# Gate steps of a PEER layer: both one-hots in one tile, a ring of three blocks, one of them taken from the weights' low parts

## The chip, the core and the metric

The kernel runs on one core of a Trainium2 chip. The metric is device time in microseconds for one execution. The profile names the engines PE (matrix products), PEld (its weight loads), DVE (vector), ACT (scalar), POOL (GpSimd) and SP (whose queue issues most loads).

## The reference

One decoder layer for 1024 prompt tokens and 64 sample tokens: RMSNorm, one input projection that feeds a retention group and an RWKV-7 group, an output projection, then a PEER mixer and a gated per-layer embedding (PLE). The part that the change touches is the PEER mixer:

```python
q = (xb @ wq).reshape(PEER_BLOCK, PEER_HEADS, 2, PEER_DKEY // 2)
s = jnp.einsum('phcd,hcnd->phcn', q, keys).astype(jnp.float32)
sv, si = lax.top_k(s, PEER_TOPK)
cand = sv[:, :, 0, :, None] + sv[:, :, 1, None, :]
cv, ci = lax.top_k(cand.reshape(PEER_BLOCK, PEER_HEADS, PEER_TOPK * PEER_TOPK), PEER_TOPK)
e = (jnp.take_along_axis(si[:, :, 0], ci // PEER_TOPK, axis=-1) * PEER_NKEYS
     + jnp.take_along_axis(si[:, :, 1], ci % PEER_TOPK, axis=-1))
gsm = jax.nn.softmax(cv, axis=-1)
hval = jnp.einsum('pd,phkd->phk', xb, u_tab[e])
act = (jax.nn.gelu(hval.astype(jnp.float32), approximate=False) * gsm).astype(xb.dtype)
return jnp.einsum('phk,phkd->pd', act, v_tab[e])
```

Every token picks 8 x 16 = 128 of 16384 experts. An expert's number is a pair (i, j) of two numbers below 128.

## The kernel before

The tokens are nine tiles of up to 128. Five of them (`E0` = 0, 1, 8 and `G1` = 2, 3) go the sparse way: `gather` (L1131) fetches 128 rows of `pu` and then 128 rows of `pv` for each token by indirect DMAs that POOL issues (L1141), and DVE multiplies and adds them (L1155, L1169). The other four (`G2` = 4, 5, 6, 7, together 512 tokens) go the dense way: all 16384 experts are computed for all of them, and a gate, zero for most pairs, picks.

The dense way has these parts.

- `hidden` (L1270) is one of 128 units, one for each number i. SP loads a block `uraw` of 128 x 1024 (L1274, ring `UB` = 2). `split` (L296) makes a high part `uh` on ACT (L298) and a low part `ul` on POOL (L302), each from a ring of `DW` = 4 blocks of 4 KB a partition. `mm3` (L324) makes the product in three passes of eight: high by high (L327), high by low of the tokens (L328), and last low by high (L330), which is the one reader of `ul`. A gelu goes on to `gd` in DRAM for the first `NPRE` = 96 units, or stays in PSUM for the others.
- `gates` (L1241) makes the gate matrix of a tile, 32 steps for each of four tiles, so 128 steps. A step (L1253 to L1262) takes four tokens. DVE builds two one-hots of 128 x 512, `oh[0]` for the first number of the pair and `oh[1]` for the second (L1256), ACT scales the four parts of `oh[0]` by the softmax (L1258), PE multiplies the two for each token into a PSUM tile `pwt` (L1261, ring of 2, each product two records), and ACT evacuates it into `wst` (L1262). After 16 steps `wst` goes to `wd` in DRAM (L1268); the last half stays on chip. The one-hots come from two tags, `oh0` and `oh1`, with two blocks of 2 KB each, in the pool `gw`.
- `dense_fused` (L1322) runs the last 32 units and multiplies each by its gate (`act`, L1284: L1292 and L1293 on DVE, which need all gate steps done) and by `pv` (`dense`, L1299: products `py`, L1312 to L1315, whose `vh` and `vl` come from ACT and POOL). `dense_stored` (L1341) does the same for the 96 stored units. Beside it `ple_weights` (L1361) loads the weights of the last stage, PLE, into the blocks that the units' rings leave.

The pool `da` (L1485, L1486) holds the rings `uh`, `ul` and `uraw`: 4 + 4 + 2 = 10 blocks of 4 KB. The same rings serve `c_query` (L1009), which runs before the gates, and the last `c_rows` (L574), which puts eight blocks of `w_out` into them.

The loop at L1525 sets the program order: for each dense tile its `topk` (L1044) side by side with the gate steps of the tile before, then a share of the 96 units, then the next tile's gates are set up. `topk` and `gather` of tile 2 are written in its second turn, those of tile 3 in its fifth. The order on each engine is then made by the framework's scheduler, which takes the operations in this order as a priority, runs them against a simulated timeline and lets an engine take what is ready there (L1566). On the chip each engine and each DMA queue works through its list in that fixed order, and a block is handed on when its last reader is done (`reuse_waits="tile"`).

Of the kernel before, what the change touches and what calls it, by code (L numbers as in the profile page):

```python
# [17 lines left out]
D = 1024  # L18
# [159 lines left out]
E0 = [0, 1, 8]  # L178
G1 = [2, 3]
DW = 4  # L180
CN = 2
BORDER = [1, 8, 2, 3, 4, 5, 6, 7]
A0 = [0, 1]
# [29 lines left out]
class K:  # L213
# [360 lines left out]
    def c_rows(self, wp, t, ring=4, da=None, x=None):  # L574

        nc, I = self.nc, self.I
        n = SIZE[t]
        half = lambda name: wp.tile([128, 512], F32, name=name, tag="x2k", bufs=ring)
        cs = [slice(0, 512), slice(512, 1024)]
        if da is not None:  # L580
            ws = []
            for k in range(8):
                ws.append(da.tile([128, D], F32, name="cw", tag=("uh", "ul")[k % 2], bufs=DW))
                nc.sync.dma_start(ws[k], I['w_out'][k])
        if da is not None:
            h = da.tile([128, D], F32, name="ch", tag="uraw", bufs=UB)
        else:
            h = wp.tile([128, D], F32, name="ch", tag="sr", bufs=1)
        nc.sync.dma_start(h[:n], I['x'][t * 128:t * 128 + n])
        yield  # L590
        ot = [half("cot"), self.tail if t == 7 else half("cot")]
        oT = [wp.tile([128, 4, 128], F32, name="coT", tag="qm", bufs=2) for _ in range(2)]
        for k in range(1 if t == 7 else 2):
            nc.sync.dma_start(ot[k][:n], self.od[t][:n, cs[k]])
        yield
        for k in range(2):
            p = self.ps("etr", "a").rearrange("p (a b) -> p a b", a=4)
            for j in range(4):
                nc.tensor.transpose(p[:, j, :n], ot[k][:n, j * 128:j * 128 + 128], self.c("ident")[:n, :n])
            nc.scalar.activation(oT[k][:, :, :n], p[:, :, :n], AF.Copy)  # L600
            yield
        if da is not None:
            p = [self.ps("ewo", "b") for _ in range(2)]
            for k in range(8):
                for c in range(2):
                    nc.tensor.matmul(p[c][:n], oT[k // 4][:, k % 4, :n], ws[k][:, cs[c]], start=k == 0, stop=k == 7)
            for c in range(2):
                nc.vector.tensor_tensor(h[:n, cs[c]], p[c][:n], h[:n, cs[c]], op=OP.add)
        else:
            for c in range(2):  # L610
                p = self.ps("ewo", "a")
                for k in range(8):
                    w = half("cw")
                    nc.sync.dma_start(w, I['w_out'][k, :, cs[c]])
                    nc.tensor.matmul(p[:n], oT[k // 4][:, k % 4, :n], w, start=k == 0, stop=k == 7)
                    if k % 4 == 3:
                        yield
                nc.vector.tensor_tensor(h[:n, cs[c]], p[:n], h[:n, cs[c]], op=OP.add)
        nc.scalar.dma_start(self.hd[t][:n], h[:n])
        junk = wp.tile([128, D], BF, name="csq", tag="x2k", bufs=ring)  # L620
        ssq = wp.tile([128, 1], F32, name="cssq")
        nc.scalar.activation(junk[:n], h[:n], AF.Square, accum_out=ssq[:n])
        r = self.rsq(wp, ssq, n, 1.0 / D, 1e-6, 1, "crs")
        gr = [half("cgr") for _ in range(2)]
        o = ROWS['norm_ffn'][0]
        for c in range(2):
            nc.sync.dma_start(gr[c], I['rows'][o + 512 * c:o + 512 * c + 512].partition_broadcast(128))
            nc.vector.scalar_tensor_tensor(h[:n, cs[c]], h[:n, cs[c]], r[:n], gr[c][:n], op0=OP.mult, op1=OP.mult)
        if x is not None:
            self.split_T(h, n, x[0], x[1], 0)  # L630
        else:
            nc.scalar.dma_start(self.xd[t][:n], h[:n])
        self.rowed.add(t)
        yield
# [374 lines left out]
    def c_query(self, wp, da, parts):  # L1009

        nc, I = self.nc, self.I
        for hc in range(16):
            kT = wp.tile([128, 128], F32, name="keysT")
            nc.sync.dma_start(kT, I['keysT'][:, hc])
            raw = da.tile([128, 8, 128], F32, name="wqr", tag="uraw", bufs=UB)
            nc.sync.dma_start(raw, I['wq'][hc])
            wh = da.tile([128, 8, 128], F32R, name="wqh", tag="uh", bufs=DW)
            wl = da.tile([128, 8, 128], F32R, name="wql", tag="ul", bufs=DW)
            self.split(wh, wl, raw, "g")
            for tiles, x in parts:  # L1020
                off, n = spans(tiles)
                s = wp.tile([128, len(tiles), 128], F32, name=f"ss{tiles[0]}", bufs=SB)
                p = self.ps("pq", "b")
                self.mm3(p[:, :n], lambda k: wh[:, k, :], lambda k: wl[:, k, :], lambda k: x[0][:, k], lambda k: x[1][:, k], 8)
                qT = wp.tile([128, n], F32, name=f"qT{tiles[0]}", bufs=1)
                nc.scalar.activation(qT, p[:, :n], AF.Copy)
                p = self.ps("psc", "a")
                for i, t in enumerate(tiles):
                    nc.tensor.matmul(p[:SIZE[t], i * 128:i * 128 + 128], qT[:, off[t]:off[t] + SIZE[t]], kT, start=True, stop=True)
                nc.scalar.activation(s, p[:, :len(tiles) * 128].rearrange("p (t k) -> p t k", k=128), AF.Copy)  # L1030
                for i, t in enumerate(tiles):
                    self.pick(self.found[t], hc, s[:, i], 128)
            yield
# [204 lines left out]
        for t in E0[1:]:  # L1238
            yield from self.gather(wp, t, rows + ("xT",) * (t == E0[-1]), acc=self.acc)

    def gates(self, wp, t):  # L1241
        nc = self.nc
        n, o = SIZE[t], self.off[t]
        p = self.ps("pit", "i").rearrange("p (a b) -> p a b", a=4)
# [5 lines left out]
        for s in range(0, n, 64):  # L1250
            last = (o + s) // 64 == self.ntok // 64 - 1
            st = self.stage[(o + s) // 64 % 2].tile([128, 128, 64], F32, name="wst", bufs=1)
            for b in range(0, 64, 4):  # L1253
                oh = [wp.tile([128, 4, 128], F32, name=f"oh{j}", bufs=2) for j in range(2)]
                for j in range(2):
                    nc.vector.tensor_tensor(oh[j], io, p[:, j, s + b:s + b + 4, None].to_broadcast([128, 4, 128]), op=OP.is_equal)  # L1256
                for j in range(4):
                    nc.scalar.activation(oh[0][:, j], oh[0][:, j], AF.Copy, scale=it[:, s + b + j:s + b + j + 1])  # L1258
                pw = self.ps("pwt", "w").rearrange("p (a b) -> p a b", a=4)
                for j in range(4):  # L1260
                    nc.tensor.matmul(pw[:, j, :], oh[1][:, j, :], oh[0][:, j, :], start=True, stop=True)  # L1261
                nc.scalar.activation(st[:, :, b:b + 4].rearrange("p i t -> p t i"), pw, AF.Copy)  # L1262
                yield
            if last:
                self.wl = st
                return
            for q in range(0, 128, WQ):
                nc.scalar.dma_start(self.wd[(o + s) // 64, :, q:q + WQ], st[:, q:q + WQ])  # L1268

    def hidden(self, dp, ep, x, i1):  # L1270
# [2 lines left out]
        raw = dp.tile([128, 8, 128], F32, name="uraw", bufs=UB)  # L1273
        nc.sync.dma_start(raw, I['puT'][i1])  # L1274
        uh = dp.tile([128, 8, 128], F32R, name="uh", bufs=DW)
        ul = dp.tile([128, 8, 128], F32R, name="ul", bufs=DW)
        self.split(uh, ul, raw, "g")
        p = self.psh.tile([128, self.ntok], F32, name="ph")
        self.mm3(p, lambda k: uh[:, k, :], lambda k: ul[:, k, :], lambda k: x[0][:, k], lambda k: x[1][:, k], 8)
# [81 lines left out]
    def ple_weights(self, cx, da, dl):  # L1361
        nc, I = self.nc, self.I
        kc = self.ntok // 128
        names = [n for n, b in (("uraw", UB), ("uh", DW), ("ul", DW)) for _ in range(b)]
        self.pg, self.pp = [], []
        for j in range(2):
            a = cx.tile([128, kc, 1024], F32R, name="pga", tag=f"cx{j}")
# [2 lines left out]
        for r, n in ((self.pp, 2), (self.pg, 8)):  # L1370
            for k in range(n):
                for j in range(2):
                    if len(r[j]) <= k:
                        if names:
                            tag = names.pop()
                            r[j].append(da.tile([128, 1024], F32R, name="pgb", tag=tag, bufs=UB if tag == "uraw" else DW))
                        else:
                            r[j].append(dl.tile([128, 1024], F32R, name="pgx", bufs=2))
        for w, src, n in ((self.pp, 'pproj', 2), (self.pg, 'pgate', 8)):
# [57 lines left out]
    def build(self):  # L1437
# [3 lines left out]
        with self.es:  # L1441
# [41 lines left out]
            cx = sb("cx2", ex)  # L1483
            x = self.rows_of(cx, G2)
            da = sb("dna", eg, bufs=2)  # L1485
            self.layout(da, [("uh", [128, 8, 128], F32R, DW), ("ul", [128, 8, 128], F32R, DW), ("uraw", [128, 8, 128], F32, UB)])  # L1486
            tp = sb("tk", et)
            self.found = {t: (tp.tile([128, 16, 16], F32, name=f"sv{t}"), tp.tile([128, 16, 16], U32, name=f"si{t}")) for t in G1 + G2}
            self.e12 = {}
# [26 lines left out]
            with ExitStack() as e:  # L1516
# [1 line left out]
                self.psh = self.pool("psumh", bufs=3, space=PS, es=e, reuse_waits="tile")  # L1518
                gw = sb("gw", e, side="right")
                self.stage = (gw, kp)  # L1520
                self.layout(gw, [("oh0", [128, 4, 128], F32, 2), ("oh1", [128, 4, 128], F32, 2), ("it", [128, 128], F32, 2)])
                gh = sb("gh", e, bufs=2, side="right")
                gate = iter(())
                nh = 0
                for i, t in enumerate(G2 + [None]):  # L1525
# [5 lines left out]
                    while nh < NPRE * (i + 1) // (len(G2) + 1):  # L1531
                        self.nc.scalar.dma_start(self.gd[nh], self.hidden(da, gh, x, nh))
                        nh += 1
                    gate = self.gates(gw, t) if t is not None else gate
                    for t in G1:
                        if i == TK1[t]:
                            run(self.topk(tp, t))
# [32 lines left out]
```

## Time and profile before

| | us |
|---|---|
| median of three runs | 3825.01 |
| lowest and highest of them | 3814.94, 3841.18 |
| the profiled execution's own time | 3810.91 |
| its span, first to last instruction | 3809.0 |

| engine | busy us | share of the span |
|---|---|---|
| PE | 3309.1 | 87% |
| PEld | 2745.7 | 72% |
| DVE | 2966.1 | 78% |
| ACT | 1228.1 | 32% |
| POOL | 2368.8 | 62% |

The shares are means over stages with different limits, so the profile is read by stage. Times inside the execution count from the first instruction. A row of a stage gives the busy time of each engine in it. A row of a group gives its busy time and the mean of one instruction in ns, then the idle time of the engine just before such instructions and what ended it. A row of the timeline gives start, length, engine, line and operation, and in brackets the idle time before it and its end. Matmuls overlap, so one takes longer than the distance to the next. The gate steps lie between 2084 and 2700 us, with a pause from 2165 to 2290. The first 96 units lie between 1940 and 2610 us, the others end at 3019 us.

### The profile page before, as it was taken

What the parts mean: (1) busy time and instruction counts of PE and PEld (TensorE: products, weight loads), DVE (VectorE), ACT (ScalarE), POOL (GpSimd) and SP (SyncE); (2) the same over time, 40 slices, a digit from 0 to 9 for tenths busy, and PEclk for the clock granted to TensorE, in tenths of its full rate; (3) what the DMA queues carried; (4) which work ended last, traced back from release to release, by engine and by line L of the source; (5) the groups of instructions that cost most, each with busy time, mean ns of one, the idle gap of its engine ahead of it and who ended that gap; (6) DMA issues with size and microseconds to landing.
All of it is one profiled execution on the core that took longest, in us unless ns stands there. A gap on an engine that the chain in (4) does not pass through costs nothing. (4 is left out here: it accounts for less than half of the span.)

```text
span 3809.0 us, 52675 instructions
## 1 busy us (share of the span) xinstructions
PE 3309.1 (87%) x17749; PEld 2745.7 (72%) x17749; DVE 2966.1 (78%) x5858; ACT 1228.1 (32%) x2273; POOL 2368.8 (62%) x2059
## 2 busy tenths in 40 slices
PE   7799995868769978875998999998799989899979
PEld 7698994645747757664887778887688877677857
DVE  5454488878897798876998978977877877788885
ACT  4232221111112111211333626778433333333322
POOL 5363176445465375545469898875688788877740
PEclk9799995668878567877999999998899999999989
DMA  7266568889878878888678889898999999999972
GB/s 253 77 221 213 175 197 293 272 296 325 262 245 312 309 265 289 281 305 311 199 271 310 299 296 321 302 361 320 328 346 334 345 371 362 365 366 351 339 247 74
DMA packets 429896, 1086.23 MB, mean 285 GB/s; under 512 B 46971, under 2 KB 146041, under 8 KB 424954
## 3 DMA queue, kind: packets, MB, share of 16 engines
q0 software_dynamic: 165888, 604.05, 44.9%
q1 hardware_dynamic: 205406, 382.77, 30.7%
q10 hardware_dynamic: 58332, 96.03, 6.9%
q8 instruction: 141, 2.31, 0.2%
q14 instruction: 129, 1.06, 0.1%
HBM read 986.68 MB, written 95.94 MB: 284 GB/s over the span
## 5 line engine op out<-in xcount | busy, mean ns | idle before, releaser
L1141 POOL DMA_INDIRECT grow<-in_pv,eid x576 | 572.8, 994 | 465.3 <-DVE gacc L1169 258.9
L1141 POOL DMA_INDIRECT grow<-in_pu,eid x576 | 571.9, 993 | 413.4 <-DVE grow L1155 228.0
L1169 DVE SCALAR_TENSOR_TENSOR gacc<-grow,ac,gacc 128x1024 f32<-128x1024 f32 x571 | 731.6, 1281 | 61.9 <-DMA grow<-in_pv,eid 55.9
L1155 DVE SCALAR_TENSOR_TENSOR grow<-grow,gacc 128x1024 f32<-128x1024 f32 x576 | 690.0, 1211 | 91.5 <-DMA grow<-in_pu,eid 87.9
L1312 PE MATMUL py<-ah,vh 128*128 128x512 f32 x1024 | 405.9, 397 | 31.5 <-ACT vh L298 21.9
L327 PE MATMUL ph<-cx,uh 128*128 128x512 f32 x1024 | 410.9, 401 | 12.6 <-ACT geh L1281 6.9
L328 PE MATMUL ph<-cx,uh 128*128 128x512 f32 x1024 | 407.2, 398 | 0.0
L1313 PE MATMUL py<-al,vh 128*128 128x512 f32 x1024 | 402.9, 394 | 2.9 <-DVE al L300 2.7
L302 POOL TENSOR_TENSOR vl<-vraw,vh 128x640 fp32r<-128x640 f32 (+2 forms) x224 | 326.2, 1461 | 39.9 <-ACT vh L298 21.9
L302 POOL TENSOR_TENSOR ul<-uraw,uh 128x1024 fp32r<-128x1024 f32 x128 | 307.7, 2404 | 60.3 <-ACT uh L298 50.8
L1315 PE MATMUL py<-ah,vl 128*128 128x512 f32 x1024 | 275.5, 400 | 16.7 <-POOL vl L302 15.6
L330 PE MATMUL ph<-cx,ul 128*128 128x512 f32 x1024 | 260.3, 393 | 6.0 <-POOL ul L302 6.0
L1312 PEld LDWEIGHTS py<-ah,vh 128*128 128x128 f32 x1024 | 194.6, 190 | 82.9 <-ACT vh L298 28.8
L298 ACT ACTIVATE vh<-vraw 128x640 fp32r<-128x640 f32 (+2 forms) x224 | 154.6, 693 | 306.9 <-PE py L1313 94.4
L1315 PEld LDWEIGHTS py<-ah,vl 128*128 128x128 f32 x1024 | 193.2, 190 | 66.8 <-POOL vl L302 24.7
L327 PEld LDWEIGHTS ph<-cx,uh 128*128 128x128 f32 x1024 | 196.5, 192 | 58.3 <-ACT uh L298 8.8
L1319 DVE TENSOR_TENSOR yT<-yT,py 128x512 f32<-128x512 f32 x216 | 147.4, 683 | 105.8 <-PE py L1315 80.4
L1313 PEld LDWEIGHTS py<-al,vh 128*128 128x128 f32 x1024 | 194.3, 190 | 47.2 <-DVE al L300 5.5
L328 PEld LDWEIGHTS ph<-cx,uh 128*128 128x128 f32 x1024 | 196.3, 192 | 40.0
L330 PEld LDWEIGHTS ph<-cx,ul 128*128 128x128 f32 x1024 | 190.7, 189 | 46.5 <-POOL ul L302 7.9
L298 ACT ACTIVATE uh<-uraw 128x1024 fp32r<-128x1024 f32 x128 | 135.6, 1059 | 253.2 <-DMA uraw<-in_puT 134.1
L1256 DVE TENSOR_TENSOR oh<-csta,pit 128x512 f32<-128x512 f32 x256 | 161.3, 679 | 49.3 <-PE pwt L1261 42.6
(402 smaller groups left out, 7422.9 us busy)
## 6 DMA issues: line engine op xcount, KB each, us to landing
uraw<-in_puT SPq DMA_DIRECT2D x128, 512.0 KB
vraw<-in_pvd SPq DMA_DIRECT2D x152, 320.0 KB
cw<-in_w_out SPq DMA_DIRECT2D x128, 256.0 KB
wd<-wst ACTq DMA_DIRECT2D x28, 1024.0 KB
wt<-wd SPq DMA_DIRECT2D x64, 448.0 KB
wraw<-in_w_ret SPq DMA_DIRECT2D x48, 512.0 KB
ewq<-in_wq SPq DMA_DIRECT2D x48, 512.0 KB
gd<-geh ACTq DMA_DIRECT2D x96, 256.0 KB
```

The costliest lines, as they stand in the source:

```text
L298: nc.scalar.activation(hi, src, AF.Copy)
L302: nc.gpsimd.tensor_tensor(lo, src, hi.bitcast(F32), op=OP.subtract)
L327: mm(out, lh(k), rh(k), start=first and k == 0, stop=False)
L328: mm(out, *((ll(k), rh(k)) if right else (lh(k), rl(k))), start=False, stop=False)
L330: mm(out, *((lh(k), rl(k)) if right else (ll(k), rh(k))), start=False, stop=last and k == nk - 1)
L1141: nc.gpsimd.indirect_dma_start(out=g, out_offset=None, in_=src, in_offset=bass.IndirectOffsetOnAxis(ap=self.eid[t][:, j:j + 1], axis=0))
L1155: nc.vector.scalar_tensor_tensor(g[:, c], g[:, c], 1.0, x[:, c], op0=OP.mult, op1=OP.mult, accum_out=hv[:, i, j:j + 1])
L1169: nc.vector.scalar_tensor_tensor(y[:, c], g[:, c], ac[:, j:j + 1], y[:, c], op0=OP.mult, op1=OP.add)
L1256: nc.vector.tensor_tensor(oh[j], io, p[:, j, s + b:s + b + 4, None].to_broadcast([128, 4, 128]), op=OP.is_equal)
L1312: nc.tensor.matmul(p, vh[:, b, :], ah, start=b == 0, stop=False)
L1313: nc.tensor.matmul(p, vh[:, b, :], al, start=False, stop=False)
L1315: nc.tensor.matmul(p, vl[:, b, :], ah, start=False, stop=b == nb - 1)
```

## The change

Both one-hots of a step become one tile of 4 KB, `oh`, of shape 128 x 2 x 4 x 128. Two such blocks lie in `gw`, in the room of the four smaller ones. Every third step takes a third block, tag `spare`, from `da`. `da` gives up one block of `ul` for it: `LW` = 3 in place of `DW` = 4. So `ul` is a ring of three everywhere that it is used: in `hidden`, in `c_query`, and in the last `c_rows`, whose eighth `w_out` block goes to `spare`. `ple_weights` takes `spare` as the first of its ten blocks.

```diff
+LW = 3
...
-                ws.append(da.tile([128, D], F32, name="cw", tag=("uh", "ul")[k % 2], bufs=DW))
+                ws.append(da.tile([128, D], F32, name="cw", **(dict(tag="spare", bufs=1) if k == 7 else dict(tag=("uh", "ul")[k % 2], bufs=(DW, LW)[k % 2]))))
...
-            wl = da.tile([128, 8, 128], F32R, name="wql", tag="ul", bufs=DW)
+            wl = da.tile([128, 8, 128], F32R, name="wql", tag="ul", bufs=LW)
...
-    def gates(self, wp, t):
+    def gates(self, wp, t, extra):
...
-                oh = [wp.tile([128, 4, 128], F32, name=f"oh{j}", bufs=2) for j in range(2)]
+                if self.turn % 3 == 2:
+                    oh = extra.tile([128, 2, 4, 128], F32, name="oh", tag="spare", bufs=1)
+                else:
+                    oh = wp.tile([128, 2, 4, 128], F32, name="oh", bufs=2)
+                self.turn += 1
                 for j in range(2):
-                    nc.vector.tensor_tensor(oh[j], io, p[:, j, s + b:s + b + 4, None].to_broadcast([128, 4, 128]), op=OP.is_equal)
+                    nc.vector.tensor_tensor(oh[:, j], io, p[:, j, s + b:s + b + 4, None].to_broadcast([128, 4, 128]), op=OP.is_equal)
                 for j in range(4):
-                    nc.scalar.activation(oh[0][:, j], oh[0][:, j], AF.Copy, scale=it[:, s + b + j:s + b + j + 1])
+                    nc.scalar.activation(oh[:, 0, j], oh[:, 0, j], AF.Copy, scale=it[:, s + b + j:s + b + j + 1])
                 pw = self.ps("pwt", "w").rearrange("p (a b) -> p a b", a=4)
                 for j in range(4):
-                    nc.tensor.matmul(pw[:, j, :], oh[1][:, j, :], oh[0][:, j, :], start=True, stop=True)
+                    nc.tensor.matmul(pw[:, j, :], oh[:, 1, j, :], oh[:, 0, j, :], start=True, stop=True)
...
-        ul = dp.tile([128, 8, 128], F32R, name="ul", bufs=DW)
+        ul = dp.tile([128, 8, 128], F32R, name="ul", bufs=LW)
...
-        names = [n for n, b in (("uraw", UB), ("uh", DW), ("ul", DW)) for _ in range(b)]
+        bufs = dict(uraw=UB, uh=DW, ul=LW, spare=1)
+        names = [n for n in bufs for _ in range(bufs[n])]
...
-            self.layout(da, [("uh", [128, 8, 128], F32R, DW), ("ul", [128, 8, 128], F32R, DW), ("uraw", [128, 8, 128], F32, UB)])
+            self.layout(da, [("uh", [128, 8, 128], F32R, DW), ("ul", [128, 8, 128], F32R, LW), ("uraw", [128, 8, 128], F32, UB), ("spare", [128, 8, 128], F32, 1)])
...
-                self.layout(gw, [("oh0", [128, 4, 128], F32, 2), ("oh1", [128, 4, 128], F32, 2), ("it", [128, 128], F32, 2)])
+                self.turn = 0
+                self.layout(gw, [("oh", [128, 2, 4, 128], F32, 2), ("it", [128, 128], F32, 2)])
```

More of the change, by code (lines that the diff above doesn't have):

```diff
@@ L1375, in ple_weights @@
                             tag = names.pop()
-                            r[j].append(da.tile([128, 1024], F32R, name="pgb", tag=tag, bufs=UB if tag == "uraw" else DW))
+                            r[j].append(da.tile([128, 1024], F32R, name="pgb", tag=tag, bufs=bufs[tag]))
                         else:
@@ L1533, in build @@
                         nh += 1
-                    gate = self.gates(gw, t) if t is not None else gate
+                    gate = self.gates(gw, t, da) if t is not None else gate
                     for t in G1:
```

## The prediction

> **What bounds the kernel now.** I read the page first, then busy time by stage, then the gate steps (L1253 to L1262) in those stages, then who waits for whom, and last the timeline around one hidden unit (`hidden`, L1270).
>
> ```profile
> span 3809.0 us, 52675 instructions
> 2080.00:2170.00 90.00, 85.84 (x441) 71.29 (x440) 88.95 (x163) 60.64 (x126) 80.39 (x59) 1.00 0.90 308
> 2170.00:2290.00 120.00, 106.33 (x441) 83.79 (x440) 96.18 (x191) 34.84 (x46) 100.42 (x70) 0.97 0.84 283
> 2290.00:2440.00 150.00, 140.85 (x729) 119.26 (x727) 134.78 (x257) 106.83 (x211) 129.60 (x98) 0.99 0.90 316
> 2440.00:2635.00 195.00, 193.00 (x1053) 166.85 (x1052) 148.67 (x237) 149.85 (x318) 129.68 (x92) 0.99 0.94 345
> 2635.00:2708.00 73.00, 43.19 (x203) 38.05 (x202) 64.22 (x108) 56.90 (x134) 33.55 (x31) 0.66 0.89 311
> 2708.00:3020.00 312.00, 311.81 (x1349) 254.76 (x1349) 240.89 (x286) 95.25 (x141) 257.84 (x214) 0.99 0.95 335
> 3020.00:3640.00 620.00, 576.08 (x2426) 457.46 (x2424) 500.59 (x802) 227.64 (x380) 491.78 (x412) 0.98 0.99 357
> ```
>
> The columns are the stretch, its length, busy time of PE, PEld, DVE, ACT and POOL, the granted PE clock, the DMA share and GB/s. Call 2440 to 2635 stage E, 2635 to 2708 stage F, 2708 to 3020 stage H (`dense_fused`). In E and H PE has no room: 193.00 of 195 and 311.81 of 312 us. In F it is busy 43.19 of 73 us, at a clock of 0.66. F is the hole: the hidden units have run out, and the dense product cannot begin until the last gate step is done. Two rows give the steps of E and F (columns PE, PEld, ACT; the count behind ACT is the evacuations, one a step):
>
> ```profile
> 2440.00:2635.00 195.00, 55.22 (x422) 54.12 (x421) 57.75 (x53) 0.99 0.94 345
> 2635.00:2708.00 73.00, 42.24 (x201) 37.55 (x200) 26.43 (x26) 0.66 0.89 311
> ```
>
> 53 steps fall into E and 26 are left for F. What holds them back in E and F together (groups of instructions, 2440 to 2708):
>
> ```profile
> L1256 DVE TENSOR_TENSOR oh<-csta,pit 128x512 f32<-128x512 f32 x152 | 95.6, 681 | 46.4 <-PE pwt L1261 41.1 <-PE ph L328 3.2 <-ACT it L1248 2.0
> L1258 ACT ACTIVATE oh<-oh,it 128x128 f32<-128x128 f32 x309 | 96.6, 390 | 17.1 <-issue 7.9 <-DVE oh L1256 4.7 <-DVE grow L1155 4.4
> L1262 ACT ACTIVATE wst<-pwt 128x512 f32<-128x512 f32 x79 | 84.2, 1087 | 32.4 <-PE pwt L1261 30.0 <-PE ph L328 1.4 <-issue 0.3
> ```
>
> DVE stood 41.1 us in front of a one-hot because PE had not yet read the old contents of its block: the ring of two. One turn of it, on PE, then DVE, then ACT:
>
> ```profile
> 2525.81 1.98 PE L330 MATMUL ph<-cx,ul 128*128 128x512 f32 x8
> 2530.35 1.95 PE L1261 MATMUL pwt<-oh,oh 128*128 128x128 f32 x16
> 2533.06 1.99 PE L330 MATMUL ph<-cx,ul 128*128 128x512 f32 x8
> ```
>
> ```profile
> 2531.44 2.48 DVE L1256 TENSOR_TENSOR oh<-csta,pit 128x512 f32<-128x512 f32 x4 [2.03 <-PE pwt L1261]
> ```
>
> ```profile
> 2523.50 1.10 ACT L1262 ACTIVATE wst<-pwt 128x512 f32<-128x512 f32 x1 [0.92 <-PE pwt L1261]
> ...
> 2531.44 1.10 ACT L1262 ACTIVATE wst<-pwt 128x512 f32<-128x512 f32 x1 [1.80 <-PE pwt L1261]
> ```
>
> From one low product (L330) to the next are 2533.06 - 2525.81 = 7.25 us: one hidden unit and two steps (16 matmuls are two steps). DVE builds two steps, waits for PE, builds two. ACT, which scales and evacuates, stands idle for 1.80 us of its turn of 2531.44 - 2523.50 = 7.94 us. The last steps and the way into H:
>
> ```profile
> 2618.22 1.95 PE L1261 MATMUL pwt<-oh,oh 128*128 128x128 f32 x16
> 2697.24 2.07 PE L1261 MATMUL pwt<-oh,oh 128*128 128x128 f32 x8 [1.31 <-ACT oh L1258]
> 2707.05 1.22 PE L1312 MATMUL py<-ah,vh 128*128 128x512 f32 x2 [7.74 <-ACT ah L298]
> ```
>
> ```profile
> 2699.35 1.02 ACT L1262 ACTIVATE wst<-pwt 128x512 f32<-128x512 f32 x1 [1.30 <-PE pwt L1261]
> ```
>
> The last evacuation ends at 2699.35 + 1.02 = 2700.4, and PE is back at 2707.05, 6.7 us later.
>
> **The change, part by part.**
>
> *Third block.* The counts stay: per step two compares, four scalings, eight matmul records, one evacuation. Only the reach grows: a compare waits for the matmuls three steps back. First the floor. PE needs in E and F its 193.00 us of E plus F's 26 steps at E's price of 1.95/2 = 0.98 us each, 25 us: 218 us. ACT needs 149.85 + 56.90 = 207 us, DVE 148.67 + 64.22 = 213 us. All three fit into 218 us where 268 are spent, so the most to win is 50 us. Then the turn: ACT is busy 7.94 - 1.80 = 6.1 us of it (the 0.92 lies before it), for one hidden unit and two steps. By the group rows a step costs ACT at most (96.6 + 84.2)/79 = 2.3 us; overlaps taken off, about 2.0. A turn with three steps then asks 6.1 + 2.0 = 8.1 us of ACT and 7.25 + 0.98 = 8.2 us of PE, 2.7 us a step if neither ever waits. If ACT stays at 87%, half way between E's share (149.85/195 = 77%) and 97%, the turn is 8.1/0.87 = 9.3 us, 3.1 a step. I take the middle, 2.9, where E now spends 195/53 = 3.7. From 2440 on 79 steps take 79 x 2.9 = 229 us, so the last evacuation ends at 2669 instead of 2700.4: 31 us earlier. Ends: -50 us, and 0 if the pace does not change.
>
> What is late next: the two PSUM tiles of `pwt`. A third step's matmuls wait for the first step's evacuation, and behind them on PE stand hidden units. Nothing more is charged, since that evacuation is in the 2.3 us.
>
> *Ring of low parts, three blocks.* The split on POOL (L302) now waits for the low product (L330) three units back, not four. Behind it on POOL stand the gather issues and the products of `topk`; DVE waits for both. Counted in order, it binds in two places. First at 2125 to 2165:
>
> ```profile
> 2153.42 2.38 POOL L302 TENSOR_TENSOR ul<-uraw,uh 128x1024 fp32r<-128x1024 f32 x1
> ```
>
> ```profile
> 2156.47 1.17 PE L330 MATMUL ph<-cx,ul 128*128 128x512 f32 x4
> ```
>
> This is unit 35, and the low product of unit 32 ends at 2156.47 + 1.17 = 2157.64, so the split would come 4.2 us later. It is the longest of five such (units 32 to 36). Bounds: 0, if the scheduler puts gather issues into the holes, and 5 x 4.2 = 21 us, if POOL (80.39 of 90 us busy there) hands on every one. I take 6, nearer to 0, since PE has two finished units in hand at that place. The second place is H, where today's ring of four is already full:
>
> ```profile
> 2796.58 1.97 PE L330 MATMUL ph<-cx,ul 128*128 128x512 f32 x8
> 2807.60 1.97 PE L330 MATMUL ph<-cx,ul 128*128 128x512 f32 x8
> ```
>
> ```profile
> 2798.69 2.41 POOL L302 TENSOR_TENSOR ul<-uraw,uh 128x1024 fp32r<-128x1024 f32 x1 [0.25 <-issue]
> ...
> 2790.77 0.33 SPq L1274 DMA_DIRECT2D uraw<-in_puT  x1
> 2807.80 1.06 ACT L298 ACTIVATE uh<-uraw 128x1024 fp32r<-128x1024 f32 x1 [3.91 <-issue]
> ...
> 2232.64 0.33 SPq L1274 DMA_DIRECT2D uraw<-in_puT  x1
> 2239.66 1.06 ACT L298 ACTIVATE uh<-uraw 128x1024 fp32r<-128x1024 f32 x1 [8.48 <-DMA uraw<-in_puT]
> ```
>
> The turn there is 2807.60 - 2796.58 = 11.02 us. Each split moves back by one turn, and with it the load that reuses its raw block. Today 2807.80 - 2790.77 = 17.0 us lie between a load's issue and the first use; 6.0 would be left. A load that ACT did wait for took 2239.66 - 2232.64 = 7.0 us, so ACT would stand about 1 us a turn. ACT is busy 95.25 of 312 us there and PE works on units split two turns (22 us) before. I charge 0; without that cover it is 1 us x 25 units (those whose split starts in H, counted) = 25 us.
>
> *One tile in place of two*, and *the two blocks that move in `ple_weights` and in the last `c_rows`*: the same operations, the same ten blocks. Both one-hots of a step were released by the same last matmul already. 0; the cover is that the spare block's holders on both sides lie hundreds of us from the gates, and there is none to lose.
>
> **Whether the 31 us reach the end.** H has PE full, so it shifts whole. The stage after has the DMA share at 0.99, but its loads shift with it. The gather of tile 3 must still be done in time:
>
> ```profile
> 3700.19 1.28 DVE L1169 SCALAR_TENSOR_TENSOR gacc<-grow,ac,gacc 128x1024 f32<-128x1024 f32 x1
> ```
>
> ```profile
> 3753.23 0.32 SPq L1405 DMA_DIRECT2D py<-yd  x1
> ```
>
> Its last row is added at 3701.5 and its sum is fetched at 3753.2, 52 us later, so 31 us go through.
>
> **Sum.** -31 + 6 + 0 + 0 = -25 us. The profiled execution took 3810.9 us, 1.9 more than its span, and would take 3786; the median of the three runs, 3825.0, is 14.1 above it, so I forecast 3800 us. From the ends, -50 and +21, come 3775 and 3846.
>
> **The rivals.**
>
> *Full catch-up.* ACT runs near 97%, all 79 steps are spread under the hidden units, and F vanishes. For it: ACT's idle time in the turn ends with PE's matmuls, which a third block covers. Against: the gather rows stand before the one-hots on DVE. 3825 - 50 + 0 to 6: about 3778.
>
> *No change.* PE is full in E, so a step that comes earlier there only pushes a hidden unit later, and F is as short of ACT as before. For it: F's ACT is busy 56.90 of 73 us; against: the 41.1 us of DVE, of which a part lies in F, and 30 us of PE idle in F that pushed hidden units would fill. 3825 + 0 to 6: 3828. The Trainium skill's page Perfetto Trace Analysis, section Optimization Strategy, says that a gap that repeats on the engine that should be saturated can mean that a buffer is lacking. In E the engine that is saturated has no such gap, only DVE has; by that rule the third block's term in E would be 0 and this rival would be the forecast. I go by the rows of F, where PE does stand.
>
> *Slower: the loads in H.* The one mechanism is the 6.0 us left between a load's issue and its use. ACT can be late by about the 5.3 us that PE spends on a hidden unit (7.25 less 1.95 for two steps) before PE lacks a `vh`, so it decides from a load of some 11.3 us on. Loads of 14 us would cost 2.7 us in each of 25 turns, 68 us: 3825 - 25 + 68 = 3868. For it: the DMA share is 0.95 in H and was 0.84 where the 7.0 us were read. Against: PE is two turns ahead.
>
> **How the numbers follow.** Forecast (3785 to 3815) 0.46, full catch-up (3768 to 3785) 0.20, no change (3815 to 3846) 0.22, slower (above 3846) 0.12. The range is 3770 to 3846: the bounds of the sum, with 5 us below for the scatter of the runs. Something over 1% (38 us) is what a measurement of this kernel can tell from no change: faster than that, below 3787, is full catch-up and a part of the forecast's lower edge, 0.28; slower, above 3863, is most of its rival, 0.10; within it 0.62.
>
> **What would show it.** Right: between 2440 and the first `py` PE is busy throughout, batches of 24 `pwt` matmuls stand where 16 do, DVE's wait for `pwt` falls from 41.1 to under 20 us, and the first `py` starts near 2676 to 2682. Wrong on the third block: batches of 16 remain and F stays above 60 us. Wrong on the ring: POOL's splits wait for L330 for more than 21 us in all before 2440, or PE shows waits for `vh`, `vl` or `uh` in H. Wrong on the way to the end: `py` starts earlier, and the stage after 3020 grows by as much.

## The result and the profile after

| | before | after |
|---|---|---|
| median of six runs, us | 3824.99 | 3784.6 |
| lowest and highest, us | 3808.06, 3841.18 | 3769.62, 3793.62 |
| the profiled execution's own time, us | 3810.91 | 3785.29 |
| its span, us | 3809.0 | 3783.5 |

The ratio is 0.9892, with a 95% interval of 0.987 to 0.9915: 41 us less, between 33 and 50. A second set of runs of the same kernel gave 0.99 (0.9869 to 0.9931), 38 us less. The two profiled executions differ by 25.6 us only. That this is the forecast's sum is chance: in the second pair of profiles below the spans differ by 61.2 us.

In the changed kernel the lines behind the one-hots are shifted: the compare is L1261, the scaling L1263, the gate product L1266, the evacuation L1267; the split is L299 and L303, the low product L331, the first `py` L1317. The busy time by stage, in the stretches of the prediction:

```profile
2440.00:2635.00 195.00, 188.20 (x1052) 161.33 (x1051) 169.99 (x267) 163.57 (x352) 135.73 (x101) 1.00 0.88 324
2635.00:2708.00 73.00, 64.22 (x316) 54.45 (x315) 49.13 (x86) 46.69 (x93) 46.33 (x36) 0.93 0.95 346
2708.00:3020.00 312.00, 312.00 (x1361) 255.28 (x1360) 247.84 (x301) 96.49 (x148) 261.43 (x216) 1.00 0.97 339
3020.00:3640.00 620.00, 557.77 (x2362) 443.19 (x2361) 497.74 (x797) 225.36 (x372) 487.09 (x411) 0.97 1.00 359
```

F, the hole, is nearly closed: PE is busy 64.22 of 73 us where it was 43.19, at a clock of 0.93 where it was 0.66. E has got small gaps, 6.8 us. The groups that held the steps back, in the same window from 2440 to 2708:

```profile
L1261 DVE TENSOR_TENSOR oh<-csta,pit 128x512 f32<-128x512 f32 x143 | 90.0, 680 | 22.3 <-issue 7.3 <-ACT oh L1263 5.9 <-ACT uh L299 4.5
L1263 ACT ACTIVATE oh<-oh,it 128x128 f32<-128x128 f32 x287 | 89.9, 392 | 16.8 <-DVE oh L1261 13.0 <-issue 3.0 <-ACT geh L1286 0.4
L1267 ACT ACTIVATE wst<-pwt 128x512 f32<-128x512 f32 x74 | 78.8, 1103 | 10.9 <-PE pwt L1266 7.8 <-issue 2.7 <-ACT geh L1286 0.4
```

DVE's 41.1 us in front of `pwt` are gone from the row. ACT's wait for `pwt` fell from 30.0 to 7.8 us. Seen from PE, the gate products of the whole phase of the units, before and then after:

```profile
L1261 PE MATMUL pwt<-oh,oh 128*128 128x128 f32 x1024 | 154.6, 301 | 37.4 <-ACT oh L1258 34.4 <-DVE oh L1256 1.9 <-PE ph L328 0.6
```

```profile
L1266 PE MATMUL pwt<-oh 128*128 128x128 f32 x1024 | 137.9, 282 | 20.3 <-ACT oh L1263 15.2 <-ACT wst L1267 5.1
```

PE stood 17 us less in front of them, and the same 1024 records took 17 us less themselves (154.6 - 137.9): fewer of them ran in the hole, at its low clock. Now part of the wait is for an evacuation of the two PSUM tiles (5.1 us), the wait that the prediction named as next. In front of the units' own products PE stood longer than before: 21.3 us at the first of the three passes, where it was 12.6, and 8.3 us at the low product, where it was 6.0.

### The profile page after: what moved, and what is told of

Its sections match the earlier page's. It is cut to its first block, busy times and chain, and to the rows that moved or that the text cites. A ratio compares the mean times of both kernels' runs of the same rounds, so it can differ in the third digit from the quotient of the medians.

```text
span 3783.5 us, 52729 instructions
## 1 busy us (share of the span) xinstructions
PE 3297.9 (87%) x17749; PEld 2733.3 (72%) x17749; DVE 2964.3 (78%) x5858; ACT 1227.5 (32%) x2273; POOL 2374.5 (63%) x2059
## 5 line engine op out<-in xcount | busy, mean ns | idle before, releaser
L1317 PE MATMUL py<-ah,vh 128*128 128x512 f32 x1024 | 403.7, 396 | 29.2 <-ACT vh L299 29.0
L328 PE MATMUL ph<-cx,uh 128*128 128x512 f32 x1024 | 409.5, 400 | 21.3 <-ACT uh L299 14.9
L303 POOL TENSOR_TENSOR vl<-vraw,vh 128x640 fp32r<-128x640 f32 (+2 forms) x224 | 326.3, 1462 | 36.6 <-ACT vh L299 27.3
L303 POOL TENSOR_TENSOR ul<-uraw,uh 128x1024 fp32r<-128x1024 f32 x128 | 308.6, 2412 | 62.7 <-ACT uh L299 32.6
L331 PE MATMUL ph<-cx,ul 128*128 128x512 f32 x1024 | 261.1, 394 | 8.3 <-POOL ul L303 8.1
L1317 PEld LDWEIGHTS py<-ah,vh 128*128 128x128 f32 x1024 | 193.4, 189 | 81.1 <-ACT vh L299 38.8
L299 ACT ACTIVATE vh<-vraw 128x640 fp32r<-128x640 f32 (+2 forms) x224 | 154.8, 692 | 291.2 <-DMA vraw<-in_pvd 112.3
L331 PEld LDWEIGHTS ph<-cx,ul 128*128 128x128 f32 x1024 | 189.7, 188 | 50.7 <-POOL ul L303 12.5
L299 ACT ACTIVATE uh<-uraw 128x1024 fp32r<-128x1024 f32 x128 | 135.4, 1058 | 188.8 <-DMA uraw<-in_puT 142.4
L303 POOL TENSOR_TENSOR wl<-wraw,wh 128x1024 fp32r<-128x1024 f32 x45 | 116.4, 2586 | 115.4 <-ACT wh L299 95.6
```

Source lines behind the costliest of these rows:

```text
L299: nc.scalar.activation(hi, src, AF.Copy)
L303: nc.gpsimd.tensor_tensor(lo, src, hi.bitcast(F32), op=OP.subtract)
L328: mm(out, lh(k), rh(k), start=first and k == 0, stop=False)
L331: mm(out, *((lh(k), rl(k)) if right else (ll(k), rh(k))), start=False, stop=last and k == nk - 1)
L1317: nc.tensor.matmul(p, vh[:, b, :], ah, start=b == 0, stop=False)
```

## A pair of profiles with the same start

The changed kernel's hidden units began at 1957.5 us, the old one's at 1939.7. So both kernels were profiled once more.

Neither has an edit.

> The kernel before, once more, for a second profiled execution. In the first one the first product ph began at 1939.7 us, in the kernel with the merged tile and a ring of four low parts at 1943.5, and in the four kernels with a ring of three low parts at 1954 to 1961, with the same order of instructions on PE until 1900 us. Theory (this is where the granted clock happens to fall in an execution, and no effect of the ring): ratio 1.000, and a first ph anywhere from 1939 to 1961. Rival (the ring of three costs some 15 us before the hidden units begin): first ph at 1939 to 1946 again.

> The changed kernel, once more. Ratio 0.987 to 0.9915 again. Theory (chance of the clock): first ph anywhere from 1939 to 1961; from there to the end 1825 to 1832 us. Rival (the ring of three costs some 15 us early): first ph at 1954 to 1961 again.

The kernel before gave 3822.53 us, ratio 1.0006 (0.9982 to 1.0029), and its first `ph` came at 1965.1. The kernel after gave 0.99 (0.9869 to 0.9931), and its first `ph` came at 1940.2. So the 17.8 us of the first pair belong to the execution, not to the ring. From its first `ph` to the end the kernel after took 1840.1 us this time, more than the 1825 to 1832 that I had expected. The delays of the late starts arise at about 1200 us. The same stretch of the kernel before, in its first and its second execution (columns as in the prediction; the third from the end is the granted clock):

```profile
1150.00:1550.00 400.00, 347.65 (x1876) 285.70 (x1875) 337.10 (x749) 69.68 (x152) 220.06 (x217) 0.73 0.84 291
```

```profile
1150.00:1550.00 400.00, 344.86 (x1726) 280.52 (x1725) 317.43 (x713) 61.09 (x138) 204.27 (x203) 0.68 0.81 277
```

PE is as busy, but at a clock of 0.68 in place of 0.73 it gets through 150 records fewer. In the two executions of the kernel after the clock in this stretch was 0.69 (the late start) and 0.74 (the early one). That leaves the first execution of before and the second of after as a pair with the same start, 1939.7 and 1940.2. Before, first `ph` to 2440, to the first `py`, to the last `ph`, to the last `py`, to the end; and the same for after:

```profile
1939.70:2440.00 500.30, 463.62 (x2165) 380.63 (x2163) 444.77 (x1027) 246.16 (x443) 427.66 (x317) 0.98 0.88 302
2440.00:2707.00 267.00, 235.24 (x1253) 204.40 (x1251) 211.89 (x343) 206.12 (x450) 162.23 (x123) 0.90 0.92 337
2707.00:3019.00 312.00, 311.76 (x1345) 254.46 (x1346) 241.49 (x287) 95.30 (x142) 258.11 (x214) 0.99 0.95 335
3019.00:3639.30 620.30, 576.99 (x2430) 458.27 (x2428) 500.28 (x801) 228.22 (x381) 491.85 (x413) 0.98 1.00 357
3639.30:3809.00 169.70, 140.24 (x639) 109.68 (x638) 109.25 (x144) 44.92 (x82) 38.33 (x56) 0.92 0.46 146
```

```profile
1940.20:2440.00 499.80, 463.52 (x2209) 382.70 (x2209) 448.04 (x1026) 261.08 (x487) 413.83 (x310) 0.98 0.88 303
2440.00:2687.50 247.50, 231.05 (x1255) 197.88 (x1255) 202.89 (x320) 193.54 (x409) 162.52 (x116) 0.98 0.91 334
2687.50:2985.20 297.70, 297.70 (x1298) 243.55 (x1297) 232.06 (x279) 89.61 (x136) 252.07 (x207) 1.00 0.96 337
2985.20:3606.60 621.40, 578.70 (x2430) 461.24 (x2428) 500.38 (x809) 232.68 (x383) 491.92 (x413) 0.98 1.00 358
3606.60:3780.30 173.70, 141.12 (x639) 110.00 (x638) 130.52 (x163) 43.76 (x82) 63.37 (x75) 0.92 0.61 201
```

The stretch from 2440 to the first `py` is 19.5 us shorter, H is 14.3 us shorter, and the rest is 5.1 us longer. H is shorter because of what was done ahead of it: 101 hidden units, counted by their records, where it was 99 before. In the order of the changed kernel two more units stand in front of the first `py`. It is so in each of the runs below that uses the third block, and in neither of the two that don't. How many steps were done at 2440 shows in the evacuations, before and after:

```profile
2084.00:2440.00 356.00, 0.00 (x0) 51.65 (x49) 0.99 0.88 304
2440.00:2708.00 268.00, 0.57 (x3) 84.18 (x79) 0.90 0.92 336
```

```profile
2084.00:2440.00 356.00, 0.00 (x0) 61.20 (x59) 0.98 0.87 303
2440.00:2708.00 268.00, 1.27 (x6) 74.24 (x70) 0.98 0.91 333
```

(The columns are DVE, ACT, clock, DMA share and GB/s; the count behind ACT is the evacuations, one a step, and 2440 falls into one of them.) 58 steps are done by 2440 and the next is being evacuated; before, 49 were done. The changed kernel is nine to ten steps ahead before the stage in which the prediction let the gain begin.

## The experiments on the change

**Merging alone, and the ring of low parts alone.**

```diff
-oh = [wp.tile([128, 4, 128], F32, name=f"oh{j}", bufs=2) for j in range(2)]
+oh = wp.tile([128, 2, 4, 128], F32, name="oh", bufs=2)
```

> Both one-hots of a step are one tile, in a ring of two blocks as before; the low parts keep their ring of four and nothing else moves. Theory (the third block is what pays): as before, ratio 0.997 to 1.003, about 3825 us; DVE waits 35 to 45 us for the gate products and PE stands about 30 us in the hole before the first py. Rival (the merged tile and the order that follows from it pay): ratio 0.993 or less.

```diff
-                if self.turn % 3 == 2:
+                if False:
```

> The changed kernel, except that the gate steps never take the third block: the one-hots go round two merged blocks, the low parts have their ring of three, and the spare block lies idle during the gates. Theory (the ring of three low parts costs next to nothing, since PE's idle time in front of the low product was 6.0 us before the change and 8.3 after it): ratio 0.999 to 1.002. My prediction's term of +6 us: 1.0016. Rival 1 (the ring costs 10 to 21 us, which the third block hides): 1.003 to 1.006. Rival 2 (holding the units back gives ACT to the gates, and this pays, not the third block): 0.995 or less.

The merged tile gave 3822.59 us, ratio 1.0005 (0.9983 to 1.0028); DVE waited 48.0 us for `pwt`, a little more than the 35 to 45 that I expected, and the phase ran as before. The ring of three low parts gave 3816.19 us, 0.9986 (0.996 to 1.0011): no cost that can be measured, and the interval leaves out both rivals (1.003 and more, 0.995 and less) and, narrowly, my term of 1.0016. DVE still stood in front of the gate products:

```profile
L1261 DVE TENSOR_TENSOR oh<-csta,pit 128x512 f32<-128x512 f32 x256 | 161.9, 680 | 54.9 <-PE pwt L1266 51.0 <-ACT it L1249 3.7
```

So neither the merging nor the ring of low parts brings the gain. The third block does. Against the run with the ring of three low parts it is worth 0.9892/0.9986 = 0.9906, about 36 us.

The ring of three is not without effect inside the phase, though. At 500.3 us after the first `ph`, which is 2440 in the first profile before, 54 steps are done in its profile, where the kernel before has 49 and the changed kernel 58 and 60. The lead does not last: the last evacuation ends 757.1 us after the first `ph`, where it was 760.7 before and is 717.7 and 721.9 in the changed kernel. PE stands longer in front of the units (the first of the three passes, before and here) and less in front of the gate products, 27.7 us in place of 37.4:

```profile
L327 PE MATMUL ph<-cx,uh 128*128 128x512 f32 x1024 | 410.9, 401 | 12.6 <-ACT geh L1281 6.9 <-ACT uh L298 5.3 <-DVE al L300 0.2
```

```profile
L328 PE MATMUL ph<-cx,uh 128*128 128x512 f32 x1024 | 410.1, 400 | 19.6 <-ACT uh L299 17.2 <-ACT geh L1286 2.3
```

**The third block in one half of the steps.**

```diff
-                if self.turn % 3 == 2:
+                if self.turn >= 64 and self.turn % 3 == 2:
```

> The changed kernel, with the third block used only by the gate steps from number 64 on, every third of them. The prediction's picture (the gain is made by the pace from 2440 us on, about steps 50 to 127): nearly all of the gain, ratio 0.989 to 0.992. Other picture (the gates gain a lead all along, most of it before step 64, where the changed kernel was already 41 us ahead if counted from the first hidden unit): about a third of the gain, 0.994 to 0.998.

```diff
-                if self.turn % 3 == 2:
+                if self.turn < 64 and self.turn % 3 == 2:
```

> The changed kernel, with the third block used only by the gate steps up to number 63, every third of them. The prediction's picture (the gain is made from about step 50 on): little, ratio 0.996 to 1.000. Other picture (the lead is built before step 64 and kept): most of the gain, 0.989 to 0.993.

Late: 3802.72 us, 0.9943 (0.9916 to 0.9971), 22 us less. Early: 3806.28 us, 0.9957 (0.9933 to 0.998), 16 us less. Neither picture holds for both: the late run lies just inside the range of the other picture, the early one between the two ranges. That 22 + 16 = 38 us is what the whole earns shows little. Each figure is uncertain by some 10 us, both runs have the ring of three low parts too, and their intervals overlap with that of the ring alone. In the profiles the last `ph` ends 1047.8 us after the start of the first with the late half and 1063.2 with the early one, where it is 1070.5 with the ring alone and 1040.8 and 1045.0 with both halves. So by single profiles the late half makes three quarters or more of what the third block brings, by the times somewhat under half, and how the gain divides stays open. From the first `ph` of each execution on, so without the chance of the clock at 1200 us (all in us, from the starts and ends in the profiles):

| kernel | first ph to first py | H (first py to last ph) | first ph to the end | longest run of gate products, records |
|---|---|---|---|---|
| before, two profiles | 767.3, 770.2 | 312.0, 312.0 | 1869.3, 1876.4 | 224 |
| merged, two blocks | 767.3 | 311.9 | 1874.4 | 224 |
| ring of three low parts, two blocks | 759.5 | 311.0 | 1868.7 | 136 |
| third block late | 750.1 | 297.7 | 1842.1 | 64 |
| third block early | 765.5 | 297.7 | 1853.3 | 112 |
| after, two profiles | 743.2, 747.3 | 297.7, 297.7 | 1826.0, 1840.1 | 40 |
| four blocks (below) | 734.6 | 297.7 | 1841.6 | 48 |

The last column counts the records of gate products that PE worked off in a row, with no product of a unit between them, in the longest such run. 224 records are 28 steps, 40 are 5. Where it is 64 or more it is the last run, the queue of steps that the units leave over; where it is 40 or 48 some 16 to 24 records more follow, with units between. The ring of three low parts alone shortens it, and the third block does so further. One row of each kernel shows what that queue costs: the gate products between 2605 and 2720, with the least, median and longest duration in ns, before and after:

```profile
L1261 PE MATMUL pwt<-oh,oh x276: 271/344/583, 2604.7 to 2698.9; 128*128 128x128 f32 x138
```

```profile
L1266 PE MATMUL pwt<-oh x192: 270/275/581, 2606.2 to 2673.8; 128*128 128x128 f32 x192
```

## What bounds the steps now

**A fourth block.**

```diff
-DW = 4
+DW = 3
...
-                if self.turn % 3 == 2:
-                    oh = extra.tile([128, 2, 4, 128], F32, name="oh", tag="spare", bufs=1)
+                if self.turn % 4 >= 2:
+                    oh = extra.tile([128, 2, 4, 128], F32, name="oh", tag="spare", bufs=2)
```

> The changed kernel with four blocks of one-hots in the ring: the high parts give one up too (rings of three high and three low parts), and two of every four steps use the two spare blocks. Theory (with three blocks DVE waits only 2.0 us for the gate products, so a fourth has nothing to take): ratio 0.988 to 0.993, and any loss shows as PE waiting for uh more than the 21.3 us of the changed kernel. Rival (the gates go on gaining a lead with each block): 0.985 or less.

3784.18 us, 0.9909 (0.9877 to 0.994): as with three. It is not that a fourth block has nothing to take, as my theory had it. The first `py` comes 734.6 us after the first `ph`, 9 to 13 us sooner than with three. PE does not wait more for `uh` either: 14.3 us, where it was 14.9 and 16.4 with three. In front of the gate products it now waits mostly for the evacuation of the two PSUM tiles, 15.9 of 18.8 us, where that was 5.1 of 20.3. What is won is given back behind the units: from the last `ph` to the end it took 809.3 us, against 785.1 and 795.1.

**Less work for ACT.**

```diff
+some = self.turn > 64 and self.turn % 2 == 1
...
+nc.vector.tensor_scalar(oh[:, 0, j], self.c("iota"), p[:, 0, s + b + j:s + b + j + 1], it[:, s + b + j:s + b + j + 1], op0=OP.is_equal, op1=OP.mult)
```

> The changed kernel; in every second gate step from number 65 on, DVE makes the scaled one-hot in four instructions of 128x128 that compare and multiply (by the row of such an instruction 4 x 0.35 = 1.4 us in place of 0.68 us), and ACT's four scalings (4 x 0.39 = 1.56 us) are left out. That takes 32 x 1.56 = 50 us from ACT and gives 32 x 0.73 = 23 us to DVE between 2480 and 2675 us. Theory (ACT is what now holds the gates: 171.2 of 203 us busy between 2440 and 2643, and PE waits there for uh and oh): ratio 0.983 to 0.988, and less than 5 us of idle PE between 2440 us and the first py. Rival (DVE, busy 175.9 of those 203 us, takes over): 0.989 to 0.997.

3808.61 us, 0.9964 (0.9948 to 0.998): slower than the changed kernel, and the rival is right. An instruction that compares and multiplies took 559 ns, not the 354 that I had taken from another. The row of that one, in the kernel before:

```profile
L754 DVE TENSOR_SCALAR m<-th,kah 128x128 f32<-128x128 f32 x16 | 4.7, 354 | 0.0
```

And the one-hots here, from 2440 to the first `py`:

```profile
L1262 DVE TENSOR_TENSOR oh<-csta,pit 128x512 f32<-128x512 f32 x119 | 77.2, 687 | 5.9 <-ACT it L1249 2.4 <-issue 2.1 <-ACT wst L1271 0.9
L1265 DVE TENSOR_SCALAR oh<-csta,pit,it 128x128 f32<-128x128 f32 x128 | 62.6, 559 | 0.0
```

So DVE got 32 x (4 x 0.559 - 0.687) = 50 us more instead of 23, and was busy 255.86 of the 277.2 us from 2440 to the first `py`. PE stood idle for 20.6 of them, where my theory had less than 5. The gather of tile 3, which shares DVE with the steps, ended late. Its last row and the fetch of its sum, in this kernel:

```profile
3776.66 1.28 DVE L1170 SCALAR_TENSOR_TENSOR gacc<-grow,ac,gacc 128x1024 f32<-128x1024 f32 x1
```

```profile
3781.70 0.32 SPq L1415 DMA_DIRECT2D py<-yd  x1
```

The fetch follows the end of the row by 3.8 us, and between them lie the copy of the sum and its way to DRAM, for which SP's queue waited 10.9 us. So the gather most likely holds the end here.

**The gather behind the units.** The same two rows in the second execution of after:

```profile
3728.62 1.27 DVE L1170 SCALAR_TENSOR_TENSOR gacc<-grow,ac,gacc 128x1024 f32<-128x1024 f32 x1
```

```profile
3735.90 0.32 SPq L1411 DMA_DIRECT2D py<-yd  x1
```

Of the 52 us of slack before the change nothing is left. The 3735.90 - 3729.89 = 6.0 us are the copy of the sum and its way to DRAM, and SP's queue stood still until the sum was there. This is SP's wait for the sum's way to DRAM, in the same execution:

```profile
SPq L1411 <- DMA yd<-gy: 10.0, 1, 10.0
```

In the first execution of after this wait is 10.2 us, with four blocks it is 7.7, and in the two executions of the kernel before there is none. After the last `py` 42 sums of this gather remain, counted in the records, where 23 did: the steps run earlier and faster on DVE, and the gather's rows come later. So two kernels leave out the last 24 of the 128 rows of `pv` of tile 3, and that part of its sum.

```diff
         y = home()
+        n -= 24 * (t == 3)
```

> The changed kernel, but the gather of tile 3 leaves out the last 24 of its 128 rows of pv: 24 fewer indirect fetches and 24 fewer sums of 1.28 us on DVE, so that its sum is fetched well before PLE needs it. Theory (the late gather costs the changed kernel little: PLE took 172.7 and 173.7 us where the kernel before took 169.7 and 172.9): 0 to 6 us less than the changed kernel, ratio 0.9875 to 0.990. Rival (the gather already holds the end): 10 us less or more, 0.9865 or less.

> The kernel with four blocks, with the same 24 rows of tile 3's gather left out. With four blocks the hidden units end 1032.3 us after the first of them began, against 1040.8 and 1045.0 with three, but from there to the end it took 809.3 us against 785.1 and 795.1. Theory (the late gather takes back there what the fourth block won): it falls by 10 us or more, to 8 us or more below the short kernel with three blocks, ratio 0.985 or less. Rival (the loss lies elsewhere, in the loads of the dense stage for one): it falls like the other, and both stay within 5 us of each other.

With three blocks 3788.06 us, 0.9892 (0.9862 to 0.9923), no change: SP waits for the gather, but this costs the changed kernel nothing that the times can show. The last stage took 171.1 us there, in place of 172.7 and 173.7. With four blocks 3775.34 us, 0.9874 (0.9843 to 0.9904): less than the 0.9909 with all rows, and by the two ratios 7 us below the short kernel with three, but the intervals overlap, and 0.985 is not reached: undecided by the times. In the profiles the stretch after the last `py` went from 180.3 to 172.0 us, the dense stage before it from 629.0 to 627.5, where the changed kernel took 612.4 and 621.4. So by single profiles some 8 us of the 14 to 24 that four blocks give back go with the late gather. Why their dense stage is longer stays open. None of these kernels, with all of the computation done, is measurably faster than the change as it is.

## Why the prediction was right, and where it was off

The mechanism was right: a third block takes DVE's wait away, the steps catch up under the units, F closes, and H starts sooner. The gain was under-estimated, 25 us against a measured 41 and 38. 3784.6 and 3780.1 lie in the range, but at and below the edge at 3785, in the stretch that I had given to the full catch-up. The mechanism of that rival did not come: it had ACT near 97% busy and F gone, and ACT was busy 193.54 of the 247.50 us from 2440 to the first `py`, with PE idle for 16.5. Whether it is over 1% is left open by the intervals, which take in 0.99.

- **Third block, -31.** It measured about 36 us against the run with the ring of three low parts, so this term was mis-sized by some 5 us, less than the times can tell apart; the next term is off by more. "From 2440 on 79 steps take 79 x 2.9 = 229 us" has two errors. The gain was let begin at 2440, although the steps get ahead before it too: 58 are done by then and the next has begun, where 49 were done. About half of that lead is there with the ring of three low parts alone. And the pace after it is not 2.9 us a step: the last evacuation ends at 2662.0 (2660.9 and 1.1), (2662.0 - 2440)/69 = 3.2 us for the 69 that then remain. The end of the steps, forecast at 2669, is near the 2662 only because the two nearly cancel. What was missing is what fills the room on PE: two more units in front of the first `py`, which shortens H by 14.3 us. I had H shift whole.
- **Ring of low parts, +6.** It costs nothing that can be measured (0.9986, some 5 us less rather than 6 more). PE's wait in front of the low product went from 6.0 and 8.0 us in the two profiles before to 8.3 and 10.9 after, some 3 us; POOL's splits waited 1.3 and 1.7 us for L331 between 1930 and 2720. In front of the five splits that the prediction saw late from 2125 to 2165 no wait for the low product of more than 0.8 us shows. The cost that does show, PE's wait for `uh` (5.3 us in both profiles before, 14.9 and 16.4 after), was not in the prediction; in the times the shorter wait in front of the gate products makes up for it.
- **Ring of low parts in H, 0, and the slower rival.** H is 297.70 us with PE busy 297.70. The loads never come too late, and the rival falls.
- **Merging, 0.** 1.0005.
- **The way to the end.** 20.0 us (the first `py`) and 14.3 (H) are won up to the last `ph`; the dense stage takes 1.1 and PLE 4.0 us more, where two executions of the kernel before differ by 1.0 and 3.2 (620.3 and 621.3, 169.7 and 172.9). The slack of 52 us was there in the kernel before, but some 4 of them are the copy of the sum and its way to DRAM. What the change does to it was not foreseen: it is gone, since the rows of the gather gave way to the one-hots on DVE.
- **No change.** It falls with F. By the rule of the Trainium skill's page Perfetto Trace Analysis, section Optimization Strategy, a gap that repeats on the engine that should be saturated can mean that a buffer is lacking. That no such gap means no missing buffer is not in the rule; I had made it of it. The trace of before had the repeating gap on DVE, and on PE only one hole of 30 us, later; the runs show that the buffer was missing all the same.
- **The signs.** DVE's wait for `pwt` fell below 20 us, as said: 2.0 and 3.8 us in all of the phase, in the two executions. PE was not busy throughout between 2440 and the first `py`: it stood idle for 247.50 - 231.05 = 16.5 us, where it was 31.8 before. Batches of 24 did not come: in the records after there are 68 batches of 8 and 26 of 16, where there were 54 and 17. With a third block most of the steps come one by one, every 2.6 to 3.1 us in this stretch (second execution of after):

```profile
2524.98 1.05 PE L1266 MATMUL pwt<-oh 128*128 128x128 f32 x8
...
2527.56 1.16 PE L1266 MATMUL pwt<-oh 128*128 128x128 f32 x8 [0.15 <-ACT wst L1267]
...
2530.63 1.05 PE L1266 MATMUL pwt<-oh 128*128 128x128 f32 x8
```

The first `py`, forecast at 2676 to 2682, came at 2687.5 with the same start, for the two units more in front of it.

## What to carry to other kernels

Where two streams share an engine and one must be done before the next stage, look for the queue that is left over when the other ends: here a deeper ring shortened it from 28 steps to 5, and the next stage began sooner by that. What fills the hole may also be work of the next stage, which then is shorter, as H was here. And a stream that gets its turn sooner on a shared engine pushes another back: work out that one's slack after the change, not before it.

## What was not expected of the hardware

The same kernel before began its hidden units at 1939.7 us in one execution and at 1965.1 in the other. These are 25 of the 32 us by which the two executions differ, and most of them are lost between 1150 and 1550 us, where the granted clock was 0.73 in the one and 0.68 in the other. A profiled pair is compared from behind such a stage, or much of its difference may be chance. A gate product that took 275 ns (median) under the units, in the kernel after, took 344 in the window with the hole, in the kernel before, where the granted clock of F was 0.66 against 0.93. So here the hole cost more than its idle time. And 128 x 128 on DVE took 559 ns as a compare and multiply by two scalars, one of them in PSUM, where 354 ns had been read from another such instruction of this kernel, with both scalars in SBUF. What makes the difference is not shown.
